# Gate's token shift through two identity products in PSUM, decay scan fed from PSUM, and new costs in the instruction scheduler

## The chip, the cores and the metric

The kernel runs on one core of a Trainium2 chip. A core has five engines with a queue of instructions each: PE multiplies matrices into PSUM (its weight loads are shown apart as PEld), DVE, ACT and POOL do elementwise work, SP issues the DMAs. Each engine takes its instructions strictly in the order in which they were written for it, and waits where an input isn't there yet. The metric is the device time of one execution in microseconds (us).

## The reference: what is computed

Two sequences of 512 and 256 tokens with 1024 channels go through the same two layers: a Mamba-2 layer and an RWKV-7 layer. The change touches the second only. Its parts that matter here:

```python
u = x @ w_in
u = u + (_token_shift_centred(u) - u) * mu        # 0.5 * (prev + next)
r, k, v = u[..., :R_DIM], ...
g = jax.nn.silu(u[..., 3 * R_DIM:4 * R_DIM])
...
w_log = -softplus(-(w0 + tanh(lw) @ w_up)) - 0.5
decay = exp(-exp(w_log))
...
out = (y + bonus) * g
```

The decays are multiplied along the tokens of a chunk; the kernel does that as a running sum of their logarithms.

## The kernel before, in words

The tokens of both sequences lie side by side (768 columns), the channels on the 128 partitions. All big products are split into three products of rounded parts (`mm3`, L144 to L146).

**Mamba stage** (up to about 760 us). It isn't edited.

**RWKV stage.** It works in 8 blocks `b` of 128 channels. For each block `rwkv_in` makes k, v, r and the gate g: a weight block is loaded and split (L125 to L127), `proj_cm` multiplies it with the input into one of two PSUM buffers `pj`, one for each sequence, and `shift_proj` does the token shift on the way out. ACT copies the buffer times `omu` = 1 - mu into SBUF (L741), and DVE adds the neighbours twice, once shifted by a token to the right and once to the left, each time reading PSUM and the SBUF result times `hmu` = mu / 2 (L743). For the gate, `omu` and `hmu` hold half of that, so that `in_g` can make silu from a tanh of the result (L840) and one more DVE instruction (L841). The gate then goes to DRAM (`sgd`) and is read again in `rwkv_final`, which multiplies it in (L1115).

`p1` goes through six windows of 256 tokens for a block. `p1_front` multiplies the low-rank parts into the PSUM bank `pl` (L873, L874), takes two tanh out of it (`ld` L877 and `ta` L878), scales `ld` in place in SBUF (L879), and DVE makes the running sum in place (the scan, L880); two exponentials follow. `pl` has one buffer. The front of a window runs one window ahead of `p1_back`, which makes the chunk matrices (L899 to L925).

`rwkv_inverse` inverts 24 triangles of 32 by 32 per block: some 60 dependent DVE instructions (L964, L965), two transposes (L967, L968), then the small products `tl` (L977), copies on ACT, the small products `px` (L987). `chain_step` runs the recurrence in 8 steps, and `rwkv_final` normalises a block's result: sums and products over `Y` on POOL (L1091 to L1101), then transposes `pf` on PE (L1105).

**What sets the order.** The order of the instructions on each engine isn't that of the code. `arrange` takes the whole program and schedules it as a list, with a cost for each instruction (`estimate`), a lag for each handover from one engine to the next (`HANDOVER`) and dependences (`trace`); it tries several settings and writes the best order found as fixed issue order. The projections of block b + 2 serve as filler on PE while block b goes through its chain. So a change of an instruction, a cost or a dependence can move instructions everywhere.

The two functions of the RWKV stage that the change edits most:

Of the kernel before, what the change touches and what calls it, by code (L numbers as in the profile page):

```python
# [14 lines left out]
F32 = mybir.dt.float32  # L15
# [3 lines left out]
AF = mybir.ActivationFunctionType  # L19
ALU = mybir.AluOpType  # L20
# [4 lines left out]
P = 128  # L25
# [16 lines left out]
DECAY = 0.5 * math.exp(-0.5)  # L42
# [6 lines left out]
def bc(ap, axis, n):  # L49
    a = ap.unsqueeze(axis)  # L50
    s = list(a.shape)
    s[axis] = n
    return a.to_broadcast(s)
# [6 lines left out]
class Trunk:  # L60
# [513 lines left out]
    def rwkv(self):  # L574
        nc, d = self.nc, self.d
        with ExitStack() as cx:
# [18 lines left out]
            self.hmu = rc.tile([P, 34], F32, name="hmu")  # L595
            nc.vector.tensor_scalar(self.omu, mu, -1.0, 1.0, op0=ALU.mult, op1=ALU.add)
            nc.vector.tensor_scalar_mul(self.hmu, mu, 0.5)
            for t in (self.omu, self.hmu):
                nc.vector.tensor_scalar_mul(t[:, 24:32], t[:, 24:32], 0.5)

            self.w0a0 = rc.tile([P, 4, RB], F32, name="w0a0")
            nc.vector.tensor_scalar_mul(self.w0a0, self.rpar[:, 0:4, :], 0.5)
# [19 lines left out]
            N = self.ring  # L622
# [110 lines left out]
    def shift_proj(self, j, out, seqs=(0, 1)):  # L733

        nc = self.nc
        ps = self.proj_cm(self.d["r_w_in"][j], seqs=seqs)
        for s in seqs:
            t0, n = SEQS[s]
            o = out[:, t0 : t0 + n]
            m = self.hmu[:, j : j + 1]  # L740
            nc.scalar.activation(o, ps[s], AF.Copy, scale=self.omu[:, j : j + 1])  # L741
            for a, p in ((o[:, 1:n], ps[s][:, 0 : n - 1]), (o[:, 0 : n - 1], ps[s][:, 1:n])):
                nc.vector.scalar_tensor_tensor(a, p, m, a, op0=ALU.mult, op1=ALU.add)  # L743
# [91 lines left out]
    def in_g(self, b):  # L835
        nc = self.nc
        g = self.t3("g")
        self.shift_proj(24 + b, g)
        th = self.t3("gth")
        nc.scalar.activation(th, g, AF.Tanh)  # L840
        nc.vector.scalar_tensor_tensor(th, th, 1.0, g, op0=ALU.add, op1=ALU.mult)  # L841
        nc.sync.dma_start(self.sgd[b], th)

# [19 lines left out]
    def p1_front(self, b, w, z, o, a, ps4, first):  # L863
        nc = self.nc
        col = lambda t, i: t[:, i, b : b + 1]
        w4 = lambda ap: ap.rearrange("p (c t) -> p c t", t=C)
        W = self.wt([P, 3, 256], "Wr")
        nc.sync.dma_start(W, self.ind[b, :, 0:3, a : a + 256])
        pl = self.pt("pl", [P, 2, 256], "pl")
        for i in range(2):  # L870
            wh, wl = self.wup
            x = self.lora_t[i][z][:, o : o + 256]
            nc.tensor.matmul(pl[:, i, :], wh[:, z, i, :], x, start=True, stop=False)  # L873
            nc.tensor.matmul(pl[:, i, :], wl[:, z, i, :], x, start=False, stop=True)  # L874
        ld = self.wt([P, 256], "ld")
        ta = self.wt([P, 256], "ta")
        nc.scalar.activation(ld, pl[:, 0, :], AF.Tanh, scale=0.5, bias=col(self.w0a0, z))  # L877
        nc.scalar.activation(ta, pl[:, 1, :], AF.Tanh, scale=0.5, bias=col(self.w0a0, 2 + z))  # L878
        nc.scalar.activation(ld, ld, AF.Copy, scale=-DECAY, bias=-DECAY)  # L879
        nc.vector.tensor_tensor_scan(ld, self.scanm, ld, 0.0, op0=ALU.mult, op1=ALU.add)  # L880
        EP = self.wt([P, 4, C + 1], "EP")
        nc.gpsimd.memset(EP[:, :, 0:1], 1.0)
        nc.scalar.activation(EP[:, :, 1:], w4(ld), AF.Exp)
        nc.scalar.activation(ld, ld, AF.Exp, scale=-1.0)
        return W, ld, ta, EP
# [197 lines left out]
    def rwkv_final(self, b, part=None):  # L1083

        nc, rw = self.nc, self.rw
        col = lambda i: self.rpar[:, i, b : b + 1]
        eng = nc.vector if b == RB - 1 else nc.gpsimd
        parts = range(3) if part is None else (part,)
        i0, n = 2 * parts[0], 2 * len(parts)
        y, sq = self.Y[:, i0 : i0 + n], self.Y[:, 6 + i0 : 6 + i0 + n]  # L1090
        eng.tensor_add(y, y, sq)  # L1091
        stat = lambda t: rw.tile([P, n, 2], F32, tag=t, bufs=1, name=t)
        mean, var = stat("gm"), stat("gv")
        nc.vector.tensor_reduce(mean, y, axis=AX.X, op=ALU.add)
        eng.tensor_scalar_mul(mean, mean, 1.0 / C)
        eng.tensor_sub(y, y, bc(mean, 3, C))
        nc.scalar.activation(sq, y, AF.Square)
        nc.vector.tensor_reduce(var, sq, axis=AX.X, op=ALU.add)
        nc.vector.tensor_scalar(var, var, 1.0 / C, GN_EPS, op0=ALU.mult, op1=ALU.add)
        rstd = self.rsqrt(rw, var, "ng")  # L1100
        eng.tensor_mul(y, y, bc(rstd, 3, C))  # L1101
        for k in parts:
            ps = self.pt("mi1", [P, 2, P], "pf")
            for i in range(2):
                nc.tensor.transpose(ps[:, i, :], self.Y[:, 2 * k + i].rearrange("p h v -> p (h v)"), self.ident)  # L1105
            o, bonus, g = (rw.tile([P, 2, P], F32, tag=t, bufs=1, name=t) for t in ("o", "bo", "sg"))
            r0, r1 = self.RGRP[k]
            tok = lambda ap: ap.rearrange("p (c t) -> p c t", t=P)[:, r0 : r1 + 1 : r1 - r0]
            oc = o.rearrange("p c (i t) -> p (c i) t", t=C)
            for i, dst in enumerate((oc[:, 0::2], oc[:, 3::-2])):  # L1110
                nc.scalar.activation(dst, ps[:, :, HR[i]], AF.Identity, scale=col(7), bias=col(8))
            nc.sync.dma_start(bonus, tok(self.bod[b]))
            nc.sync.dma_start(g, tok(self.sgd[b]))
            eng.tensor_add(o, o, bonus)
            nc.vector.tensor_mul(o, o, g)  # L1115
            if b == RB - 1:
                hi, lo = (tok(x[:, 1, :]) for x in self.x67)
                nc.scalar.copy(hi, o)
                nc.vector.tensor_sub(lo, o, hi.bitcast(F32))
            else:  # L1120
                nc.sync.dma_start(tok(self.odram[b]), o)
# [153 lines left out]
def size(ap, first=1):  # L1275
    return math.prod(int(n) for _, n in ap.ap[first:])
# [43 lines left out]
def space(t, name):  # L1320
    return str(t._space).endswith(name)


class Program:
# [49 lines left out]
    def estimate(self, i, x, src, dst):  # L1374
        e, op = self.eng[i], x.opcode
        if e == "SP":
# [4 lines left out]
            if dst:  # L1381
                n = size(dst[0], 0)
# [5 lines left out]
        if e == "PE":  # L1388
            N, M, K = size(src[0]), size(src[1]), int(src[0].ap[0][1])
# [30 lines left out]
        N = max(size(a) for a in src + dst)  # L1420
# [3 lines left out]
        ps = any(space(a.tensor, "PSUM") for a in src + dst if hasattr(a.tensor, "_space"))  # L1424
        ptr = sum(1 for a in src if size(a) == 1 and N > 1)
        two = len(src) - ptr
        if e == "DVE":
            if op != "TensorScalarPtr":
                c = (66 + N) / 0.96
                if op == "Reciprocal":  # L1430
                    c = 70 + N * 6.4
            elif x.ins and two == 1 and not ps:
                c = 69 + N / 1.92 + 61 * ptr
            else:
                c = (66 + N) / 0.96 + 61 * ptr
            if any(N > 64 and len(a.ap) > 1 and abs(int(a.ap[-1][0])) >= 16 and space(a.tensor, "SBUF") for a in src + dst):
                c += 0.78 * N
            if getattr(x, "is_tensor_tensor_scan", False):
                c = 70 + 2.07 * N
            if not ps:  # L1440
                self.lock[i] = c - 52
        elif e == "Activation":
            far = any(N > 64 and len(a.ap) > 1 and abs(int(a.ap[-1][0])) >= 16 for a in src + dst)
            c = 51 + N * (1.9 if far else 0.8333) + (0 if ps else 43) + 93.5 * ptr + (93 if len(dst) > 1 else 0)
        elif op == "Memset":
            c = 35 + 0.8333 * N
        elif op == "TensorScalarPtr":
            c = 130 + N * 0.83 + 90 * ptr
            self.lock[i] = c - 95
        elif two > 1:  # L1450
            c = 185 + 1.6 * N if N < 200 else 222 + 1.75 * N
            if str(x.outs[0].dtype) == "dt.float32r":
                c += 115
            self.lock[i] = c - 130
        else:
            c = 130 + 0.9 * N
            self.lock[i] = c - 87
        self.cost[i] = c

    def node(self, pred):  # L1460
# [7 lines left out]
    def trace(self, nc, tc, aps):  # L1468

        ins, eng = self.ins, self.eng  # L1470
# [12 lines left out]
        for i, x in enumerate(ins):  # L1483
# [17 lines left out]
            for wr, l in enumerate(aps[i]):  # L1501
                for b in l:
                    t = b.tensor
# [8 lines left out]
            for wr, nm, psum, q0, q1, bits in recs:  # L1512
                if nm in free_at:
                    pred.add(free_at[nm])
                W, R = live[nm]
                for j, a, z, m, w in chain(W, R) if wr or psum else W:
                    hit = a < q1 and q0 < z and m & bits
                    if psum or hit:
                        pred.add(j)
                        if eng[j] == eng[i] and w and hit:  # L1520
                            self.raw.add((j, i))
            for wr, nm, psum, q0, q1, bits in recs:
                W, R = live[nm]
# [409 lines left out]
```

## Time and profile before

| | |
|---|---|
| median of 3 runs | 1604.52 us (1603.03 to 1611.49) |
| the profiled execution | 1600.35 us, span 1598.5 us |
| mean granted PE clock | 0.978 |
| busy: PE, PEld, DVE, ACT, POOL | 94%, 79%, 84%, 54%, 45% |
| DMA | 161.41 MB, 101 GB/s over the span |
| chain of work that ended last | PE 67%, DVE 16%, POOL 6%, DMA 4%, ACT 3% |

How to read the lines that follow in this document. A group of instructions reads "line engine operation out<-in shape xcount | busy us, mean ns of one | idle time of the engine before them, and what ended it". A row of the timeline reads "start us, duration us, engine, line, operation, names, shape, count [idle before <- releaser]". A row of the waits reads "who waited <- for whom: us in total, times, longest". A row of the busy times by stretch reads "stretch, length, then the busy time and number of instructions of PE, PEld, DVE, ACT and POOL, the granted PE clock (1.00 is full), the share of the DMA engines, GB/s". A full fp32 product leaves two records on PE, a split one leaves one for each of its three parts. Durations overlap: a row of DVE holds some fixed time that the next instruction runs into.

### The profile page before, as it was taken

The page shows a single profiled execution, that of the slowest core. Times are in us where ns is not written, and L with a number is a line of the kernel's source. Part 1 is how long each engine was busy: PE and PEld are TensorE (multiplying, and loading weights), DVE is VectorE, ACT ScalarE, POOL GpSimd, SP SyncE. Part 2 cuts the span into 40 slices and gives each one's busy share as a digit, 9 for nine tenths or more (in the row PEclk, how much of TensorE's full clock was granted, in tenths as well). Part 3 has the DMA queues.
Part 4 walks back from the last instruction along what each step waited for, and adds up shares of the span by engine and source line. Part 5 has one row for each costly group of instructions (what it writes and reads, how often), then busy time and mean ns, then how long its engine had stood idle before and what let it go on. Part 6 is the DMA issues. An engine that isn't in the chain of part 4 may idle for free.

```text
span 1598.5 us, 39340 instructions
## 1 busy us (share of the span) xinstructions
PE 1497.7 (94%) x15210; PEld 1266.0 (79%) x15210; DVE 1340.6 (84%) x2947; ACT 857.1 (54%) x1988; POOL 712.0 (45%) x983
## 2 busy tenths in 40 slices
PE   7999999999999999999889989989999999988996
PEld 6878888888989779998768767777777777776886
DVE  6768988888978896569679788999999899989869
ACT  4245454544445453323565766757585766756342
POOL 1148574565754743000061644637283645547210
PEclk9999999999999999999989999999999999989998
DMA  5111212122012044432335334353535445345332
GB/s 174 54 46 36 78 34 67 60 70 84 28 66 80 14 139 133 134 120 80 106 106 160 111 101 140 105 149 86 149 92 141 121 114 153 100 139 156 111 114 87
DMA packets 150315, 161.41 MB, mean 101 GB/s; under 512 B 39632, under 2 KB 106928, under 8 KB 150128
## 3 DMA queue, kind: packets, MB, share of 16 engines
q1 hardware_dynamic: 150128, 158.89, 33.1%
q8 instruction: 120, 1.97, 0.5%
q14 instruction: 67, 0.55, 0.1%
HBM read 121.43 MB, written 40.55 MB: 101 GB/s over the span
## 4 chain that ended last, share of the span: by engine, by line
PE 67%; DVE 16%; POOL 6%; DMA 4%; issue 3%; ACT 3%; SPq 0%; DVEq 0%; POOLq 0%; ACTq 0%
PE pj L144 9%; PE pj L145 9%; PE pj L146 9%; PE pz L146 3%; PE pz L145 3%; PE pz L144 3%; PE po L146 3%; PE po L145 3%; PE po L144 3%; PE py L1040 2%; PE ptd L914 2%; PE pst L384 2%; PE py L423 2%; DVE tl L965 2%; DVE XN L964 2%
## 5 line engine op out<-in xcount | busy, mean ns | idle before, releaser
L144 PE MATMUL pj<-xh,whi 128*128 128x512 f32 (+1 forms) x1056 | 381.0, 361 | 20.3 <-ACT whi L126 11.7
L146 PE MATMUL pj<-xh,wlo 128*128 128x512 f32 (+1 forms) x1056 | 375.0, 356 | 1.6 <-DVE wlo L127 1.6
L145 PE MATMUL pj<-xl,whi 128*128 128x512 f32 (+1 forms) x1056 | 374.1, 354 | 1.1 <-DVE xl L140 1.1
L144 PEld LDWEIGHTS pj<-xh,whi 128*128 128x128 f32 x1056 | 205.0, 194 | 48.2 <-ACT whi L126 13.0
L146 PEld LDWEIGHTS pj<-xh,wlo 128*128 128x128 f32 x1056 | 204.4, 194 | 28.1 <-DVE wlo L127 3.0
L145 PEld LDWEIGHTS pj<-xl,whi 128*128 128x128 f32 x1056 | 204.7, 194 | 26.7 <-issue 2.7
L126 ACT CAST whi<-wraw 128x512 fp32r<-128x512 f32 x213 | 131.8, 620 | 135.2 <-PE pj L145 62.1
L127 DVE TENSOR_TENSOR wlo<-wraw,whi 128x512 fp32r<-128x512 f32 x213 | 157.9, 747 | 34.5 <-ACT whi L126 33.5
L418 POOL TENSOR_SCALAR G<-past,ddt,dt 128x128 f32<-128x128 f32 x192 | 136.0, 720 | 94.4 <-DVE ddt L324 59.2
L145 PE MATMUL po<-wlo,xh 128*128 128x256 f32 x528 | 150.7, 286 | 5.0 <-DVE wlo L127 5.0
L144 PE MATMUL po<-whi,xh 128*128 128x256 f32 x528 | 151.2, 286 | 0.1
L146 PE MATMUL po<-whi,xl 128*128 128x256 f32 x528 | 150.1, 284 | 0.0
L238 DVE SCALAR_TENSOR_TENSOR conv<-conv,convw 128x770 f32<-128x770 f32 x128 | 140.2, 1096 | 1.3
L144 PE MATMUL pz<-whi,xh 128*128 128x256 f32 x384 | 116.0, 302 | 0.4 <-DVE sz L262 0.4
L903 POOL TENSOR_TENSOR G<-EP,Wr 64x256 f32<-64x256 f32 x96 | 88.2, 919 | 51.2 <-DMA Wr<-ind 30.5
L146 PE MATMUL pz<-whi,xl 128*128 128x256 f32 x384 | 110.5, 288 | 0.0
L145 PE MATMUL pz<-wlo,xh 128*128 128x256 f32 x384 | 110.1, 287 | 0.0
L382 POOL TENSOR_TENSOR xw<-xB,dtws 128x256 f32<-128x256 f32 x64 | 54.1, 852 | 121.6 <-ACT xB L370 108.5
L145 PEld LDWEIGHTS po<-wlo,xh 128*128 128x128 f32 x528 | 100.1, 190 | 6.9 <-DVE wlo L127 5.9
L144 PEld LDWEIGHTS po<-whi,xh 128*128 128x128 f32 x528 | 100.2, 190 | 1.6 <-DVE acc L505 0.4
L146 PEld LDWEIGHTS po<-whi,xl 128*128 128x128 f32 x528 | 100.1, 190 | 1.1 <-issue 0.2
L1054 POOL TENSOR_TENSOR ZP<-SV,PC 64x128 f32<-64x128 f32 x128 | 64.9, 515 | 59.4 <-DVE SV L1066 48.4
(289 smaller groups left out, 3792.0 us busy)
## 6 DMA issues: line engine op xcount, KB each, us to landing
wraw<-in_r_w_in SPq DMA_DIRECT2D x72, 256.0 KB, 3.0
Wr<-ind SPq DMA_DIRECT2D x48, 384.0 KB, 3.8
wraw<-in_m_w_xbc SPq DMA_DIRECT2D x64, 256.0 KB, 2.8
wraw<-in_m_w_z SPq DMA_DIRECT2D x32, 256.0 KB, 2.8
wraw<-in_m_w_out SPq DMA_DIRECT2D x32, 256.0 KB, 4.6
ydram<-yst SPq DMA_DIRECT2D x16, 384.0 KB, 2.8
yraw<-ydram SPq DMA_DIRECT2D x24, 256.0 KB, 2.9
ind<-k SPq DMA_DIRECT2D x32, 192.0 KB, 3.0
```

Source lines behind the costliest of these rows:

```text
L126: nc.scalar.copy(hi, raw)
L127: nc.vector.tensor_sub(lo, raw, hi.bitcast(F32))
L144: mm(ps, ah, bh, start=first, stop=False)
L145: mm(ps, ah, bl, start=False, stop=False)
L146: mm(ps, al, bh, start=False, stop=last)
L238: nc.vector.scalar_tensor_tensor(acc, u[:, t : t + n], w[:, b, t : t + 1], acc, op0=ALU.mult, op1=ALU.add)
L382: nc.gpsimd.tensor_tensor(hv(xw), hv(xB[c][:, 0:256]), bc(self.dtws[:, c, z, hs], 2, 64), op=ALU.mult)
L384: nc.tensor.matmul(ps, xB[c][:, 256:384], xw, start=True, stop=True)
L418: nc.gpsimd.tensor_scalar(G[:, h, :], self.past, self.ddt[:, c, i : i + 1], self.dt[:, c, 0, i : i + 1], op0=ALU.mult, op1=ALU.add)
L423: nc.tensor.matmul(py[r, 64 * h : 64 * h + 64], G[:, h, r], x3[:, h, :], start=True, stop=True)
L903: nc.gpsimd.tensor_tensor(G[hr, ps4, h, 0, :], EP[hr, :, 0:C], w4(tok(W[hr, h])), op=ALU.mult)
L1054: nc.gpsimd.tensor_tensor(ZP[HR[h], :, s, :], SV[HR[h], :, s, h, :], bc(pc[s][HR[h]], 2, C), op=ALU.mult)
```

## The change

The gate's shift (and only the gate's: `j // 8 in (3,)`) takes another way. ACT copies the buffer times `hmu` into a piece `us` in SBUF. PE multiplies `us` with the identity and adds it into the same PSUM buffer, one token to the right, and again one token to the left. DVE then takes one pass: the buffer minus twice `us`. The gate is no longer halved on the way; the tanh gets a factor 0.5 and the last product in `rwkv_final` too. In `p1_front` the scaling of `ld` writes back into the bank `pl` instead of SBUF, and the scan reads it there. In the scheduler, costs of POOL instructions rise or change, and any two instructions on one engine other than PE that touch the same PSUM tile, the first of them writing, are now given the lag of a handover.

```diff
-            for t in (self.omu, self.hmu):
-                nc.vector.tensor_scalar_mul(t[:, 24:32], t[:, 24:32], 0.5)
...
+            if j // 8 in (3,):
+                u = self.inp.tile([P, n + 2], F32, tag=f"U{s}", bufs=1, name="us")[:, 0:n]
+                nc.scalar.activation(u, ps[s], AF.Copy, scale=m)
+                nc.tensor.matmul(ps[s][:, 1:n], self.ident, u[:, 0 : n - 1], start=False, stop=False, skip_group_check=True)
+                nc.tensor.matmul(ps[s][:, 0 : n - 1], self.ident, u[:, 1:n], start=False, stop=True, skip_group_check=True)
+                nc.vector.scalar_tensor_tensor(o, u, -2.0, ps[s], op0=ALU.mult, op1=ALU.add)
+                continue
...
-        nc.scalar.activation(th, g, AF.Tanh)
+        nc.scalar.activation(th, g, AF.Tanh, scale=0.5)
...
-        nc.scalar.activation(ld, ld, AF.Copy, scale=-DECAY, bias=-DECAY)
-        nc.vector.tensor_tensor_scan(ld, self.scanm, ld, 0.0, op0=ALU.mult, op1=ALU.add)
+        lp = pl[:, 0, :]
+        nc.scalar.activation(lp, ld, AF.Copy, scale=-DECAY, bias=-DECAY)
+        nc.vector.tensor_tensor_scan(ld, self.scanm, lp, 0.0, op0=ALU.mult, op1=ALU.add)
...
-            nc.vector.tensor_mul(o, o, g)
+            nc.vector.scalar_tensor_tensor(o, o, 0.5, g, op0=ALU.mult, op1=ALU.mult)
...
-            c = 35 + 0.8333 * N
+            c = 90 + 0.8333 * N
...
-            c = 185 + 1.6 * N if N < 200 else 222 + 1.75 * N
+            c = 185 + 1.6 * N if N < 200 else 240 + 1.8 * N
...
-                        if eng[j] == eng[i] and w and hit:
+                        if eng[j] == eng[i] and w and (hit or psum and eng[i] != "PE"):
```

Against before, line numbers behind L597 are lower by two, behind the gate's shift higher by five, and behind the scan higher by six (L977 is now L983).

How the order moves, at the end of the fifth inverse (the one whose `tl` starts at 1241.87 us in the profile before). PE, before: `pj_15031` and `pj_15056` are the gate's buffers for the two sequences, `pj_16118` is the next block's.

```order
L145 MATMUL pj_15056<-xl,whi 128x256
L146 MATMUL pj_15056<-xh,wlo 128x256
L144 MATMUL pj_15056<-xh,whi 128x256
L145 MATMUL pj_15056<-xl,whi 128x256
L146 MATMUL pj_15056<-xh,wlo 128x256
L977 MATMUL tl<-XN,TD 32x32 x48
L144 MATMUL pj_16118<-xh,whi 128x512
L145 MATMUL pj_16118<-xl,whi 128x512
```

PE, after the change, at the same place: `pj_15049` and `pj_15074` are the gate's buffers, `us` the scaled piece.

```order
L144 MATMUL pj_15074<-xh,whi 128x256
L145 MATMUL pj_15074<-xl,whi 128x256
L146 MATMUL pj_15074<-xh,wlo 128x256
L742 MATMUL pj_15049<-us,ident 128x511
L743 MATMUL pj_15049<-us,ident 128x511
L742 MATMUL pj_15074<-us,ident 128x255
L743 MATMUL pj_15074<-us,ident 128x255
L983 MATMUL tl<-XN,TD 32x32 x48
L144 MATMUL pj_16140<-xh,whi 128x512
L145 MATMUL pj_16140<-xl,whi 128x512
```

All four new products stand between the gate's last projection and `tl`. In the seven rounds with such a place this is so four times; in the others three, one or none of the four stand ahead of `tl` and the rest between `tl` and `px` (L993).

DVE at the same place, before, from the last transpose of the inverse on:

```order
L968 STREAM_TRANSPOSE TC<-tl 128x1024
L743 SCALAR_TENSOR_TENSOR g<-pj_15031,hmu,g 128x511
L127 TENSOR_TENSOR wlo<-wraw,whi 128x512
L743 SCALAR_TENSOR_TENSOR g<-pj_15031,hmu,g 128x511
L127 TENSOR_TENSOR wlo<-wraw,whi 128x512
L743 SCALAR_TENSOR_TENSOR g<-pj_15056,hmu,g 128x255 x2
L1115 TENSOR_TENSOR o<-o,sg 128x256
L900 TENSOR_TENSOR KB<-KB,Wr 128x2x4x64
```

DVE, after the change:

```order
L974 STREAM_TRANSPOSE TC<-tl 128x1024
L744 SCALAR_TENSOR_TENSOR g<-us,pj_15049 128x512
L127 TENSOR_TENSOR wlo<-wraw,whi 128x512
L744 SCALAR_TENSOR_TENSOR g<-us,pj_15074 128x256
L1121 SCALAR_TENSOR_TENSOR o<-o,sg 128x256
L846 SCALAR_TENSOR_TENSOR gth<-gth,g 128x768
L906 TENSOR_TENSOR KB<-KB,Wr 128x2x4x64
```

Two passes instead of four stand there, and the gate's last DVE instruction (L846) has moved up ahead of the next window's first (L906).

More of the change, by code (lines that the diff above doesn't have):

```diff
@@ L1450, in estimate @@
         elif two > 1:
-            c = 185 + 1.6 * N if N < 200 else 222 + 1.75 * N
+            c = 185 + 1.6 * N if N < 200 else 240 + 1.8 * N
             if str(x.outs[0].dtype) == "dt.float32r":
                 c += 115
-            self.lock[i] = c - 130
+            self.lock[i] = c - 170
         else:
-            c = 130 + 0.9 * N
-            self.lock[i] = c - 87
+            c = 190 + 0.9 * N
+            self.lock[i] = c - 147
         self.cost[i] = c
```

## The prediction, on record before the change was run

> **What bounds the kernel now.** I read the page's engine shares first, then the busy time by stretch, then the waits, then the timeline around one inverse.
>
> ```profile
> PE 1497.7 (94%) x15210; PEld 1266.0 (79%) x15210; DVE 1340.6 (84%) x2947; ACT 857.1 (54%) x1988; POOL 712.0 (45%) x983
> ```
>
> PE looks like the bound, but the share is an average over stages. By stretch (columns: PE, PEld, DVE, ACT, POOL busy, then granted clock, DMA share, GB/s):
>
> ```profile
> 0.00:570.00 570.00, 552.13 (x3895) 472.64 (x3896) 475.40 (x885) 267.57 (x571) 306.37 (x387) 1.00 0.20 64
> 850.00:1510.00 660.00, 610.69 (x8265) 487.06 (x8265) 599.06 (x1386) 429.63 (x1061) 332.42 (x487) 0.97 0.43 123
> 1115.20:1154.60 39.40, 35.68 (x314) 28.01 (x312) 37.34 (x115) 20.27 (x49) 9.84 (x15) 0.96 0.47 132
> 1154.60:1202.00 47.40, 46.94 (x845) 37.19 (x845) 42.39 (x73) 39.87 (x101) 34.45 (x55) 1.00 0.41 115
> 1202.00:1241.80 39.80, 35.28 (x305) 27.95 (x303) 38.01 (x116) 21.05 (x50) 11.62 (x16) 1.00 0.49 135
> 1241.80:1295.40 53.60, 52.02 (x842) 40.47 (x842) 45.48 (x76) 40.82 (x102) 39.90 (x59) 0.94 0.40 122
> ```
>
> The first row is the Mamba stage: PE 97% busy at full clock, and the change adds nothing there. The second is the RWKV loop, where all edits lie: PE 93%, DVE 91%. The other four are two of its eight rounds, each cut in two at the end of `rwkv_inverse`. During an inverse DVE is full (37.34 of 39.40, 38.01 of 39.80) and PE idles some 4 us; during the burst of windows and chain steps after it PE is full (46.94 of 47.40, 52.02 of 53.60) and DVE has 5 to 8 us to spare. So work taken from DVE pays during the inverse, and work given to PE costs in the burst. Which of the two the edits touch decides the sign.
>
> PE's idle time at the end of an inverse has two owners (us in total, times, longest):
>
> ```profile
> PE pf L1105 <- POOL Y L1101: 14.6, 7, 3.2
> PE tl L977 <- DVE TC L968: 4.7, 4, 1.8
> ```
>
> The second is the wait ahead of the `tl` products, which need the last transpose of the inverse. It is the only idle time that stands where the new products are put. One such place, PE:
>
> ```profile
> 1235.70 0.44 PE L1105 MATMUL pf<-ident,Y 128*128 128x128 f32 x2 [1.41 <-POOL Y L1101]
> ...
> 1240.30 0.28 PE L146 MATMUL pj<-xh,wlo 128*128 128x256 f32 x1
> 1241.87 2.00 PE L977 MATMUL tl<-XN,TD 32*32 32x32 f32 x96 [1.29 <-DVE TC L968]
> 1243.85 0.47 PE L144 MATMUL pj<-xh,whi 128*128 128x512 f32 x1
> 1244.15 0.40 PE L145 MATMUL pj<-xl,whi 128*128 128x512 f32 x1
> ...
> 1244.97 0.63 PE L145 MATMUL pj<-xl,whi 128*128 128x512 f32 x1
> 1245.39 0.63 PE L146 MATMUL pj<-xh,wlo 128*128 128x512 f32 x1
> ```
>
> and DVE at the same time:
>
> ```profile
> 1240.60 1.21 DVE L968 STREAM_TRANSPOSE TC<-tl 128x1024 f32<-128x1024 f32 x1
> 1241.73 0.71 DVE L743 SCALAR_TENSOR_TENSOR g<-pj,hmu,g 128x511 f32<-128x511 f32 x1
> ...
> 1244.22 0.99 DVE L743 SCALAR_TENSOR_TENSOR g<-pj,hmu,g 128x255 f32<-128x255 f32 x2
> 1245.13 0.41 DVE L1115 TENSOR_TENSOR o<-o,sg 128x256 f32<-128x256 f32 x1
> 1246.94 0.69 DVE L900 TENSOR_TENSOR KB<-KB,Wr 128x512 f32<-128x512 f32 x1 [1.39 <-DMA Wr<-ind]
> ```
>
> Here DVE does the gate's shift right behind the inverse, at the head of the burst, and then waits 1.39 us for a load.
>
> **The change part by part.** *Gate shift, DVE.* Rows: the two halves of the gate's shift, and the nearest row of the new form (SBUF and PSUM in, constant scalar, SBUF out).
>
> ```profile
> L743 DVE SCALAR_TENSOR_TENSOR g<-pj,hmu,g 128x511 f32<-128x511 f32 x16 | 11.7, 732 | 0.1
> L743 DVE SCALAR_TENSOR_TENSOR g<-pj,hmu,g 128x255 f32<-128x255 f32 x16 | 7.5, 471 | 3.2 <-ACT g L741 3.1
> L262 DVE SCALAR_TENSOR_TENSOR sz<-zth,pz 128x256 f32<-128x256 f32 x48 | 19.7, 410 | 1.3 <-ACT zth L260 1.0
> ```
>
> Removed: 11.7 + 7.5 = 19.2 us. Added: 8 of 256 columns at 410 ns and 8 of 512. A constant instead of a column of scalars is worth 471 - 410 = 61 ns, so 512 columns take about 732 - 61 = 671 ns; 8 x (671 + 410) = 8.7 us. DVE gains 10.5 us (9.6 if the 61 ns don't hold). ACT's copy is replaced one for one: 0.
>
> *Scan.* It took 759 ns on average.
>
> ```profile
> L880 DVE TENSOR_TENSOR_SCAN ld<-scanm,ld 128x256 f32<-128x256 bf16 x48 | 36.5, 759 | 3.3 <-ACT ld L879 2.8
> L442 DVE TENSOR_TENSOR yv<-yv,sz 128x256 f32<-128x256 f32 x48 | 23.6, 502 | 0.2
> L441 DVE TENSOR_TENSOR yv<-yv,py 128x256 f32<-128x256 f32 x48 | 19.8, 412 | 8.2 <-POOL yv L440 6.6 <-PE py L423 1.6
> ```
>
> The other two rows are the same product or sum of 256 columns with both inputs in SBUF (502) and with one in PSUM (412): 90 ns less. Between 0 and 90 ns for the scan, I take 83: 48 x 83 = 4.0 us (0 to 4.3). The Trainium skill, "SBUF — State Buffer", section "Who interferes with whom", gives a reason: DVE's second SBUF input comes through a read port shared with GpSimd, and an instruction with one SBUF input doesn't contend. By that rule the scan would get all of the 90 ns.
>
> Together DVE loses 14.5 us of work, 1.8 us a round. How much of it is time? The gate's part (10.5) is shed at the head of the burst, where DVE has idle time and PE none; the scans lie on both sides. I count half: -7 us (0 to -14.5).
>
> *Gate shift, PE.* Two products with the identity in full fp32 for each piece. A product of this kind leaves two records; the chain of waits shows four in 0.86 us for two products of 256 columns, so 0.43 each and 0.86 for 512; products standing alone with 64 rows take 1.05 and 0.63 (512 and 256 columns).
>
> ```profile
> 209.90 0.86 PE po L433 x4
> ...
> 85.20 1.05 PE prow L344 x2
> 87.27 0.63 PE prow L344 x2
> ```
>
> A round gets 2 x 0.86 + 2 x 0.43 = 2.58 us, eight rounds 20.6 us (26.9 at the dearer price). In the order, of the seven rounds with an inverse behind the gate, four have all four products straight ahead of `tl`, one has three (1.72), one a short one (0.43), one none; so 4 x 2.58 + 2.15 = 12.5 us stand ahead of `tl`, and 4.7 us of idle time is there to take them. The rest, 7.8 us, would make `tl` late. Those behind `tl` fill PE's wait for the copies that `px` needs: 0. What is queued behind a late `tl` is `px` and then the whole burst. But the copy out of PSUM and the sums go to PE earlier where the round's DVE work is shorter, so I take half, +4 us (0 to +7.8).
>
> *Clock.* In the PE rows above the spacing of 512-column products goes from 0.30 to 0.42 us, and their duration from 0.40 to 0.63, some 3 us after PE had stood idle for 1.41 and then 1.29 us. The burst's granted clock is 0.94 over 53.60 us: 3.2 us of PE work lost in that round; over the loop 0.03 x 660 = 20 us. Products that fill the idle time ahead of `tl` may avoid some of these drops. I take -3 us (0 to -10). The Trainium skill, "TensorE: Matmul & The Clock Gate", section "What's actually happening", has the half rate come after at least one idle window of about 3.4 us; by that rule no drop would have come here and nothing could be won. The trace disagrees: its idle pieces are shorter and the rate halves.
>
> *Wait added.* A window's `pl` bank is now held until the scan has read it, not until `ta` is made, and PE's next `pl` products stand behind that. One handover:
>
> ```profile
> 1163.11 0.48 ACT L878 ACTIVATE ta<-pl,w0a 128x256 f32<-128x256 f32 x1
> 1163.64 0.19 PEld L873 LDWEIGHTS pl<-lora,wuh 128*128 128x128 f32 x1
> 1163.92 0.69 DVE L880 TENSOR_TENSOR_SCAN ld<-scanm,ld 128x256 f32<-128x256 bf16 x1 [0.52 <-ACT ld L879]
> ...
> 1164.10 0.28 PE L874 MATMUL pl<-lora,wul 128*128 128x256 f32 x1
> ...
> 1165.00 0.47 ACT L877 ACTIVATE ld<-pl,w0a 128x256 f32<-128x256 f32 x1
> ```
>
> PE began the next window at 1163.64, 0.05 us after `ta`, and had it at 1164.38; the scan ended at 1164.61. So the next `pl` moves back by 1.0 us, to 1165.4, where ACT took it at 1165.00. The front runs one window ahead of the rest of its window, and that is the cover: 0. Without it, it is 1 us at each such handover.
>
> *The rest.* The copy into `pl` instead of SBUF, the constant in the last product with the gate, two setup multiplies: 0, none is on a full engine. The changed estimates reorder every engine. The Mamba stage can't gain, since PE is full; in the loop I put 0, between -5 and +5 us (a third of the 14.6 us that `pf` waits for POOL).
>
> Sum: -7 + 4 - 3 = **-6 us**. The profiled execution took 1600.35 us (span 1598.5), so 1594.3 for such a one; the median of the runs, 1604.5, lies 4.2 above it, so 1598.5.
>
> **The rivals.**
>
> *Full relief.* PE is late nowhere, because the clock stays up and the round is truly DVE's: all 14.5 us come off, 1590. For it: DVE's 95% during the inverses. Against it: the 1.39 us wait behind the gate's shift.
>
> *PE becomes the bound* (slower). The products sit in front of `tl` and the burst has no slack: 20.6 us added, 2 of them hidden in the 4.7, 7 won on DVE: +11.6, 1616. It decides where PE's idle time ahead of `tl` is under 2.6 us, as in every round (longest 1.8). Against it: four rounds only have all the products there.
>
> *The bank hold bites* (slower). The Trainium skill, "PSUM — Partial Sum Buffer", section "PSUM bank collisions raise a hardware error", forbids two engines in one bank and quadrant at once. In this kernel that means the `pl` products wait for the scan. If two of a round's six handovers cost 1 us and DVE delays those scans by half as much again, 8 x 2 x 1.5 = 24 us, less the 14.5 won on DVE: 1614. The trace speaks against it: even in the tight handover above ACT took the next `pl` only 0.4 us before the delayed products would end.
>
> *Nothing happens.* DVE's relief falls into its idle time and PE's products into PE's: 1604.5.
>
> **How the numbers follow.** Forecast 0.44, full relief 0.28, PE bound 0.16, bank hold 0.08, nothing 0.04. The forecast's own range is 1592 to 1606 (its terms at half their ends). A measurement tells about 0.5%, 8 us, from no change: the bounds are 1596.5 and 1612.5. Faster: full relief 0.28 and 0.3 of the forecast, 0.41. Slower: three quarters of PE bound and half of bank hold, 0.16. Same: 0.43. The range, 1586 to 1617, leaves out a fifth of full relief's cases below and the worst of both slow rivals above.
>
> **What would show it.** Right: in the loop DVE's busy time falls by 13 to 15 us and PE's idle time ahead of `tl` goes to about 0; the gate's group falls from 19.2 to 9 us; the scan from 759 to about 675 ns; the new products take 18 to 27 us of PE; the granted clock of the loop rises above 0.97. Wrong: `tl` starts over 2 us after its transpose (PE bound); PE waits for the scan at `pl` by over 10 us in total (bank hold); the Mamba stage changes by over 3 us.

## The result and the profile after

The changed kernel took 1594.68 us (median of 11 runs, 1589.23 to 1601.27), the kernel before 1603.03 in the same job (11 runs, 1599.86 to 1611.49). The ratio is 0.994, with a 95% interval of 0.9926 to 0.9954: by it 9.6 us faster, 7.4 to 11.9 (the two medians are 8.4 apart). The profiled execution took 1594.9 us, its span 1593.1. Of all runs counted here and below, one (1660.79 us, of the scan alone in the old order) was slow, at a lower granted clock (0.956), and is left out of the medians.

The first line is the busy time of the engines from the page of the changed kernel, the second its loop of rounds from the table by stretches (PE, PEld, DVE, ACT, POOL busy, then granted clock, DMA share, GB/s).

```profile
PE 1501.1 (94%) x15274; PEld 1272.7 (80%) x15274; DVE 1327.4 (83%) x2929; ACT 862.2 (54%) x1988; POOL 687.2 (43%) x983
```

```profile
850.00:1510.00 660.00, 618.61 (x8424) 495.04 (x8426) 590.26 (x1375) 436.42 (x1068) 320.29 (x487) 0.98 0.43 124
```

DVE has 13.2 us less work than before (1340.6). PE is as full as it was, with 64 more records, which are 32 products, and the loop's clock stands at 0.98 after 0.97. ACT's first copy of a token shift in the RWKV stage starts at 761.8 us (761.1 before), so the Mamba stage is no shorter. The two profiled spans differ by 5.4 us. This gain lies in the loop (its last inverse ends at 1504.6, before at 1508.2) and in the tail behind it (1.8 us shorter).

The groups of the edited lines in the loop (x14 of a product are two records each for seven rounds):

```profile
L886 DVE TENSOR_TENSOR_SCAN ld<-scanm,pl 128x256 f32<-128x256 bf16 x42 | 28.4, 676 | 1.9 <-ACT pl L885 1.6
...
L885 ACT ACTIVATE pl<-ld 128x256 f32<-128x256 f32 x42 | 16.3, 387 | 0.8
...
L743 PE MATMUL pj<-us,ident 128*128 128x511 f32 x14 | 7.3, 607 | 0.0
...
L744 DVE SCALAR_TENSOR_TENSOR g<-us,pj 128x512 f32<-128x512 f32 x7 | 4.6, 657 | 0.0
...
L743 PE MATMUL pj<-us,ident 128*128 128x255 f32 x14 | 4.3, 386 | 0.0
...
L744 DVE SCALAR_TENSOR_TENSOR g<-us,pj 128x256 f32<-128x256 f32 x7 | 2.8, 400 | 0.0
```

The scan takes 676 ns instead of 759, ACT's copy ahead of it 387 instead of 421, and the gate's sums 7.4 us in seven rounds, which is 8.5 in eight, instead of 19.2. PE's waits in the loop (us in total, times, longest):

```profile
PE pf L1111 <- POOL Y L1107: 9.0, 6, 2.8
...
PE pl L878 <- DVE ld L886: 3.2, 5, 1.6
...
PE tl L983 <- DVE TC L974: 2.1, 3, 1.5
```

The wait ahead of `tl` is down from 4.7 us and that of `pf` from 14.6, and the new wait for the scan at `pl` is small.

### The profile page after: what moved, and what is told of

Read it like the earlier page. It is cut to its first block, busy times and chain, and to the rows that moved or that the text cites. A ratio compares the mean times of both kernels' runs of the same rounds, so it can differ in the third digit from the quotient of the medians.

```text
span 1593.1 us, 39443 instructions
## 1 busy us (share of the span) xinstructions
PE 1501.1 (94%) x15274; PEld 1272.7 (80%) x15274; DVE 1327.4 (83%) x2929; ACT 862.2 (54%) x1988; POOL 687.2 (43%) x983
## 4 chain that ended last, share of the span: by engine, by line
PE 70%; DVE 16%; POOL 4%; ACT 4%; DMA 2%; issue 2%; SPq 1%; DVEq 0%; ACTq 0%; POOLq 0%
PE pj L144 10%; PE pj L145 10%; PE pj L146 10%; PE po L144 3%; PE po L145 3%; PE po L146 3%; PE pz L145 3%; PE pz L144 3%; PE pz L146 3%; PE ptd L920 3%; PE py L1046 2%; PE pst L384 2%; DVE tl L971 2%; DVE XN L970 2%; PE po L433 2%
## 5 line engine op out<-in xcount | busy, mean ns | idle before, releaser
L146 PE MATMUL pj<-xh,wlo 128*128 128x512 f32 (+1 forms) x1056 | 370.5, 351 | 7.2 <-DVE wlo L127 7.2
L418 POOL TENSOR_SCALAR G<-past,ddt,dt 128x128 f32<-128x128 f32 x192 | 127.5, 677 | 93.1 <-DVE ddt L324 60.1
L1060 POOL TENSOR_TENSOR ZP<-SV,PC 64x128 f32<-64x128 f32 x128 | 61.6, 489 | 63.8 <-DVE SV L1072 48.1
```

The lines of the kernel that those rows point to most:

```text
L146: mm(ps, al, bh, start=False, stop=last)
L418: nc.gpsimd.tensor_scalar(G[:, h, :], self.past, self.ddt[:, c, i : i + 1], self.dt[:, c, 0, i : i + 1], op0=ALU.mult, op1=ALU.add)
L1060: nc.gpsimd.tensor_tensor(ZP[HR[h], :, s, :], SV[HR[h], :, s, h, :], bc(pc[s][HR[h]], 2, C), op=ALU.mult)
```

## The experiments

At the start there were three theories. A: the operations gain, by VectorE's (DVE's) relief. B: the changed estimates gain, by the order they make. C: the identity products fill TensorE's (PE's) idle time and keep its clock up. Each run has its ratio to the kernel before on the same chip; the runs stand on three chips. "Slower" below means that the whole interval of the ratio lies above 1.

### Each part alone, in an order planned for it

Four kernels take parts of the change, and the scheduler plans each anew.

**Gate's shift alone** (scan and estimates as before):

```diff
+            if j // 8 in (3,):
...
+                nc.tensor.matmul(ps[s][:, 1:n], self.ident, u[:, 0 : n - 1], start=False, stop=False, skip_group_check=True)
+                nc.tensor.matmul(ps[s][:, 0 : n - 1], self.ident, u[:, 1:n], start=False, stop=True, skip_group_check=True)
+                nc.vector.scalar_tensor_tensor(o, u, -2.0, ps[s], op0=ALU.mult, op1=ALU.add)
```

> The kernel before with the gate's new shift alone; the scan and the estimates as they were. Theory A (the gain is VectorE's relief, the gate's shift giving most of it): VectorE's busy time over the span falls by 9 to 10.5 us, the eight gates' group from 19.2 to about 9 us, and the time falls by 4 to 7 us, to 1596 to 1599. Theory B (the gain comes from the order that the new estimates make): no gain, 1603 within 3 us, since the identity products cost TensorE what VectorE is spared. Theory C (the identity products fill TensorE's idle time and keep the granted clock up): a gain of 4 to 8 us with a loop clock above 0.97.

Measured: 1613.9 us, ratio 1.0063 (1.0041 to 1.0084). Slower.

**Scan from PSUM alone:**

```diff
-        nc.scalar.activation(ld, ld, AF.Copy, scale=-DECAY, bias=-DECAY)
-        nc.vector.tensor_tensor_scan(ld, self.scanm, ld, 0.0, op0=ALU.mult, op1=ALU.add)
+        lp = pl[:, 0, :]
+        nc.scalar.activation(lp, ld, AF.Copy, scale=-DECAY, bias=-DECAY)
+        nc.vector.tensor_tensor_scan(ld, self.scanm, lp, 0.0, op0=ALU.mult, op1=ALU.add)
```

> The kernel before with the scan's input in PSUM alone. Theory A: the scan falls from 759 to about 676 ns and ScalarE's copy ahead of it from 421 to about 387 ns, 4.0 and 1.6 us of work, and the time falls by 1 to 4 us, to 1599 to 1602. Theories B and C: no change, 1603 within 2 us. If the longer hold of the pl bank cost time, it would be slower, by 2 to 5 us.

Measured: 1609.4 us, ratio 1.0033 (1.0019 to 1.0046). Slower. The size is the one expected of a longer bank hold, but PE waits only 3.2 us in the loop for scans at `pl`, as much as in the changed kernel.

**Changed estimates alone** (only the scheduler's costs and its dependence rule):

```diff
-            c = 35 + 0.8333 * N
+            c = 90 + 0.8333 * N
...
-            c = 130 + 0.9 * N
+            c = 190 + 0.9 * N
```

> The kernel before with the changed estimates alone: the same instructions in another order. Theory A: no change, 1603 within 3 us. Theory B: the whole of the gain, 1594 to 1597, with TensorE's wait for GpSimd ahead of pf down from 14.6 to about 9 us as in the changed kernel.

Measured: 1613.5 us, ratio 1.0056 (1.004 to 1.0072). Slower, with the very instructions of the kernel before. PE's wait for POOL ahead of `pf` is 14.8 us in the loop, not the 9 that theory B expected.

**Gate's shift and scan, with the old estimates** (the edits in the scheduler undone):

```diff
-            c = 190 + 0.9 * N
+            c = 130 + 0.9 * N
...
```

> The changed kernel with the estimates put back: gate shift and scan together in an order made by the old estimates. Theory A: the whole of the gain, 1593 to 1597. Theory B: 1600 to 1603. Theory C: 1595 to 1599, with a loop clock of 0.98 against 0.97.

Measured: 1611.8 us, ratio 1.0038 (1.0025 to 1.0052). Slower.

All three theories miss here: every part alone is slower, and so are both edits without the estimates, yet the whole is 0.6% faster. What each kernel changes besides its operations is the order of everything. The same instructions in two orders differ by 9 us (estimates alone against the kernel before), the changed operations in two orders by 16 us (1.0038 against 0.994). So a part can't be judged while the scheduler plans anew. Nor does the gate's edit raise the clock in every order: over the whole program its mean is 0.970 to 0.980 in the executions of the gate alone, 0.969 to 0.979 with gate, scan and the old estimates, and 0.976 to 0.982 in the kernel before.

### Operations and order apart

The next kernels don't plan. They have an order written out as a table, taken from one of the two kernels, so that operations and order are changed one at a time:

```diff
-    for line in prog.schedule().values():
+    for line in issue_order():
```

Where an edit has other instructions than the order's own kernel, they stand in its place: the one sum where the second of the two stood, two sums where the one stood, the products where ACT's copy lands by the planned times. With the scan's input in PSUM, PE's next products into `pl` move back behind the scan where the old order has them ahead of it.

**Both edits in the order of the kernel before:**

> The operations of the changed kernel (gate shift and scan) in the issue order of the kernel before, written out as a table; the identity products stand where their copy lands, and TensorE's order gives way only where the pl bank demands it. Theory A (the operations gain, by VectorE's relief, and what each planned order is worth is another matter): 1592 to 1599. Theory B (the new order gains, the operations do not): 1601 to 1607.

Measured: 1645.0 us, ratio 1.0249 (1.0228 to 1.027). Neither range holds it.

**No edit, in the order of the changed kernel:**

> The operations of the kernel before in the issue order of the changed kernel, instruction by instruction (the two sums of each gate piece stand where the one sum stood). Theory A: no gain, 1601 to 1609. Theory B: the whole gain, 1593 to 1597.

Measured: 1610.3 us, ratio 1.0034 (1.0021 to 1.0047). Theory B falls: for the old operations the new order is worse than the old one, by 5.5 us. Theory A's range is passed by 1.3 us.

**Gate's shift alone in the order of the changed kernel:**

> The changed kernel in its own issue order with the scan put back to SBUF. Theory A, with the scan worth its 4.0 us on VectorE and 1.6 us on ScalarE times a share of half to all: 1597 to 1600. Theory B: 1594 to 1596.

Measured: 1606.0 us, ratio 1.0009 (0.9996 to 1.0022), above both ranges.

**Scan alone in the order of the changed kernel:**

> The changed kernel in its own issue order with the gate's shift put back (two sums on VectorE, no identity products). Theory A, with the gate worth 10.5 us of VectorE's work times half, less up to 4 us of TensorE's: 1597 to 1603. Theory B: 1594 to 1596.

Measured: 1604.0 us, ratio 1.0003 (0.9987 to 1.0019), 1 us above theory A's range.

**Gate's shift alone in the order of the kernel before:**

> The gate's shift alone in the issue order of the kernel before, the identity products standing where their copy lands. The run with both edits in that order took 1645.0 us. If the products do the harm there (an order that left little idle time ahead of tl), most of it is here: 1620 to 1645. If the scan does, through the pl bank, this one is near the kernel before or a little faster by VectorE's relief: 1597 to 1606.

Measured: 1617.7 us, ratio 1.0072 (1.0047 to 1.0097), between the two expectations. The busy time of the engines in this run:

```profile
PE 1515.6 (94%) x15274; PEld 1273.9 (79%) x15274; DVE 1333.9 (83%) x2929; ACT 856.8 (53%) x1988; POOL 715.5 (44%) x983
```

PE is busy 17.9 us longer than in the kernel before (1497.7) and idles only 3.4 us less (97.4 of a span of 1613.0, against 100.8 of 1598.5), so the new products aren't covered. `tl` isn't where it shows: it starts at most 1.7 us after its transpose, 3.9 us in all over eight rounds. In six of seven rounds the two short products stand behind `tl`, in four of these behind `px` too, and the seven bursts behind `tl` take 354.1 us instead of 343.0.

**Scan alone in the order of the kernel before:**

> The scan from PSUM alone in the issue order of the kernel before, which let TensorE write the next pl before the scan of the last had run; there TensorE's rows now give way. If the longer hold of the bank is what cost 40 us in the run with both edits in that order: 1625 to 1645, with TensorE's wait for the scan at pl over 10 us. If not: 1599 to 1604 by the shorter scans.

Measured: 1637.0 us, ratio 1.0198 (1.0156 to 1.0241). The longer hold of the bank is most of what costs. PE's wait for it from 850 to 1510 us shows that (the last inverse of this run ends at 1541):

```profile
PE pl L873 <- DVE ld L881: 17.9, 21, 3.4
```

PE waits 21 times for the scan, where the changed kernel waits 5 times; over the whole execution it is 21.8 us. PE idles 122.7 us in all, 21.9 more than in the kernel before. The old order let the next products into `pl` follow close behind `ta`, and now they stand behind the scan, which on average ends 2.2 us after `ta`. Put together, the ratios to the kernel before are:

| order | no edit | gate | scan | both |
|---|---|---|---|---|
| of the kernel before | 1 | 1.0072 | 1.0198 | 1.0249 |
| of the changed kernel | 1.0034 | 1.0009 | 1.0003 | 0.9940 |

In the new order the edits gain 0.94%, or 15.1 us (0.9940 / 1.0034); in the old one they lose 2.5%. Of two kernels that share this order, then, the one with the edits is faster: the gain is that of the operations in an order that was planned around them. In the new order the gate gains 4.0 us alone and 10.1 beside the scan; the scan 5.0 alone and 11.1 beside the gate. By the intervals each of these is known within about 3 us.

### What the operations gain in the new order

First, what the identity products do to PE. This is PE's timeline with no edit in the new order, third round, around `tl` (start, length, and in brackets the idle time before and who ended it):

```profile
1063.43 0.39 PE L146 MATMUL pj<-xh,wlo 128*128 128x512 f32 x1
1064.61 2.01 PE L977 MATMUL tl<-XN,TD 32*32 32x32 f32 x96 [0.80 <-DVE TC L968]
1066.55 0.44 PE L1105 MATMUL pf<-ident,Y 128*128 128x128 f32 x2
1068.83 2.02 PE L987 MATMUL px<-TC,TL 32*32 32x32 f32 x96 [1.84 <-ACT TL L980]
1072.00 0.79 PE L144 MATMUL pj<-xh,whi 128*128 128x512 f32 x1 [1.15 <-DVE g L743]
1072.59 0.63 PE L145 MATMUL pj<-xl,whi 128*128 128x512 f32 x1
1073.02 0.63 PE L146 MATMUL pj<-xh,wlo 128*128 128x512 f32 x1
```

The same place in the changed kernel:

```profile
1060.76 0.40 PE L146 MATMUL pj<-xh,wlo 128*128 128x512 f32 x1
1061.00 0.59 PE L742 MATMUL pj<-us,ident 128*128 128x255 f32 x2
1061.52 2.00 PE L983 MATMUL tl<-XN,TD 32*32 32x32 f32 x96
1063.45 0.70 PE L743 MATMUL pj<-us,ident 128*128 128x255 f32 x2
1063.99 1.02 PE L742 MATMUL pj<-us,ident 128*128 128x511 f32 x2
1064.84 1.02 PE L743 MATMUL pj<-us,ident 128*128 128x511 f32 x2
1065.70 0.38 PE L1111 MATMUL pf<-ident,Y 128*128 128x128 f32 x2
1066.01 1.99 PE L993 MATMUL px<-TC,TL 32*32 32x32 f32 x96
1067.94 0.50 PE L144 MATMUL pj<-xh,whi 128*128 128x512 f32 x1
1068.27 0.39 PE L145 MATMUL pj<-xl,whi 128*128 128x512 f32 x1
1068.50 0.40 PE L146 MATMUL pj<-xh,wlo 128*128 128x512 f32 x1
```

Without the products PE idles three times here, for 0.80, 1.84 and 1.15 us; the last of these is for the gate's second sum on DVE, which still reads the buffer. With them there is no gap: one stands ahead of `tl`, three between `tl` and `px`. Behind it the 512-column products follow each other every 0.23 us instead of every 0.43. The clock is that of the stretches: with no edit in the new order, the loop and then the 15.4 us behind `tl` of this round,

```profile
850.00:1510.00 660.00, 599.44 (x8114) 480.73 (x8113) 600.20 (x1358) 428.72 (x1055) 330.44 (x484) 0.95 0.43 122
1064.60:1080.00 15.40, 12.39 (x254) 9.81 (x258) 11.07 (x17) 12.43 (x24) 9.50 (x13) 0.67 0.60 188
```

and in the changed kernel the same stage of the round:

```profile
1060.50:1076.00 15.50, 15.50 (x307) 11.76 (x306) 11.83 (x20) 14.49 (x30) 10.14 (x15) 1.00 0.66 212
```

The clock is 0.67 against 1.00 there, and 0.95 against 0.98 over the loop. The loop of the scan alone, in the new order,

```profile
850.00:1510.00 660.00, 602.04 (x8130) 484.00 (x8129) 590.52 (x1366) 430.21 (x1055) 318.15 (x485) 0.95 0.42 122
```

and of the gate's shift alone, in the new order:

```profile
850.00:1510.00 660.00, 615.24 (x8229) 490.90 (x8229) 593.75 (x1371) 428.40 (x1057) 335.24 (x486) 0.98 0.43 123
```

In this order it is the gate's edit that brings the clock back. All executions agree: over the whole program their mean clocks are 0.967 to 0.973 with no edit, 0.967 to 0.974 with the scan alone, 0.976 to 0.982 with the gate alone and 0.979 to 0.987 with both. The busy time of the engines with no edit in the new order:

```profile
PE 1494.2 (93%) x15210; PEld 1270.3 (79%) x15210; DVE 1349.7 (84%) x2947; ACT 861.5 (54%) x1988; POOL 701.8 (44%) x983
```

In a span of 1608.2 us PE idles 114.0; in the changed kernel it idles 92.0 of 1593.1 (1501.1 busy). So the edits take away 22.0 us of its idle time, and the new products, some 20 us, make it only 6.9 us busier. Added up from the timeline, PE is idle for 21.9 us in the 8 us ahead of the eight `tl` with no edit, for 7.9 us in the changed kernel. PE's wait for `tl` alone, with no edit in the new order:

```profile
PE tl L977 <- DVE TC L968: 12.1, 5, 4.0
```

Two runs ask which half of the gate's edit counts, and how much room is left.

**Identity products doubled** (each piece is scaled with a quarter instead of half, and each product issued twice):

```diff
-                nc.scalar.activation(u, ps[s], AF.Copy, scale=m)
+                nc.scalar.activation(u, ps[s], AF.Copy, scale=self.qmu[:, j : j + 1])
                 nc.tensor.matmul(ps[s][:, 1:n], self.ident, u[:, 0 : n - 1], start=False, stop=False, skip_group_check=True)
+                nc.tensor.matmul(ps[s][:, 1:n], self.ident, u[:, 0 : n - 1], start=False, stop=False, skip_group_check=True)
+                nc.tensor.matmul(ps[s][:, 0 : n - 1], self.ident, u[:, 1:n], start=False, stop=False, skip_group_check=True)
                 nc.tensor.matmul(ps[s][:, 0 : n - 1], self.ident, u[:, 1:n], start=False, stop=True, skip_group_check=True)
-                nc.vector.scalar_tensor_tensor(o, u, -2.0, ps[s], op0=ALU.mult, op1=ALU.add)
+                nc.vector.scalar_tensor_tensor(o, u, -4.0, ps[s], op0=ALU.mult, op1=ALU.add)
```

> The changed kernel in its own issue order, each identity product issued twice in a row on half the input, the same sum. TensorE gets what it already got from the change once more, about 20 us by the prediction's price of 2.58 us a round. If the products lie in idle time of TensorE that still has room (the wait for tl): 1593 to 1598. If that room is used up and each further product delays tl and what is queued behind it: 1605 to 1615.

Measured: 1609.3 us, ratio 1.0022 (0.9997 to 1.0046), 13.2 us over the changed kernel (1.0022 / 0.9940). The room is used up. PE's timeline of the fifth round, whose `TC` was ready at 1248.2:

```profile
1248.12 1.02 PE L747 MATMUL pj<-us,ident 128*128 128x511 f32 x2
1248.97 0.59 PE L744 MATMUL pj<-us,ident 128*128 128x255 f32 x2
1249.40 0.59 PE L745 MATMUL pj<-us,ident 128*128 128x255 f32 x2
1249.83 0.59 PE L746 MATMUL pj<-us,ident 128*128 128x255 f32 x2
1250.26 0.59 PE L747 MATMUL pj<-us,ident 128*128 128x255 f32 x2
1250.79 2.00 PE L987 MATMUL tl<-XN,TD 32*32 32x32 f32 x96
```

The products stand 0.85 and 0.43 us apart, and `tl` starts 2.6 us after its transpose. Over the eight rounds `tl` is 10.0 us late, against 2.0 in the changed kernel. That is 8.0 us more; the other 5 of the 13 aren't located.

**The gate's one sum made twice** (products stay, DVE gets work back):

```diff
                 nc.vector.scalar_tensor_tensor(o, u, -2.0, ps[s], op0=ALU.mult, op1=ALU.add)
+                nc.vector.scalar_tensor_tensor(o, u, -2.0, ps[s], op0=ALU.mult, op1=ALU.add)
```

> The changed kernel in its own issue order with each gate piece's one sum on VectorE made twice in a row, the second over the first: TensorE's identity products stay, and 8 x (676 + 381) = 8.5 us of the VectorE work that the change took away come back. Theory A (relief of VectorE is what gains): most of the gate's part goes again, 1600 to 1605. Theory C (the identity products fill TensorE's idle time ahead of tl and keep its granted clock up): little goes, 1594 to 1598, and the loop's clock stays at 0.98.

Measured: 1601.0 us, ratio 0.9974 (0.9953 to 0.9996), 5.5 us over the changed kernel for 8.5 us of DVE's work. By the two intervals the 5.5 us are known within 4.1, so the share is 0.64, but anything from 0.16 to 1.1 fits. The stretch behind `tl` of the third round, in this run:

```profile
1062.00:1077.40 15.40, 15.40 (x307) 11.70 (x306) 12.89 (x21) 14.45 (x30) 9.97 (x15) 1.00 0.66 213
```

The clock stays at 1.00 here and at 0.98 over the loop, so it hangs on the products and not on DVE's relief. With the share of 0.64, the 10.5 us that the gate takes off DVE are worth 6.7, within 5; of the 10.1 us that the gate brings beside the scan, 3.4 remain for the filled gaps and the clock, less what the products cost. By these bounds that rest could be nothing. So in the new order theory A holds; of theory C the filled gaps and the clock are shown, their worth in time isn't; and B, that the order gains by itself, falls.

## Why the prediction was right or wrong

The sum was -6 us and the time fell by 9.6 (0.6% of 1603.03), to a point inside the range. Several terms under the sum do not hold.

**DVE's work, right.** 14.5 us less was forecast, 13.2 is measured over the span. The gate's group went to 8.5 us (8.7 forecast), the scan to 676 ns (676 forecast). The share, put at half, measures 0.64 for the gate's part, between 0.16 and 1.1.

**The scan's part was sized in the wrong order.** In the new order an SBUF scan would take not 759 but 810 ns, so the edit is worth 6.4 us there and not 4.0, besides 1.6 on ACT's copy, which the sum didn't have at all.

**PE's products, the price right, the cover wrong.** 2.58 us a round holds (0.85 and 0.43 us a product, above). But `tl` became late by 2.0 us in all against 1.6 before, not by 4 more. The step that failed is "4.7 us of idle time is there to take them": that counts only waits for `TC` in the order of the kernel before. By the count of all idle time in the 8 us ahead of `tl` the old order has 15.7 us, and the new one without the products 21.9. One round also differs from what the text ahead of the prediction says: where `tl` starts at 1148.94 us, none of the four products stands ahead of it, one stands between `tl` and `px`, and three stand behind `px`, 1.72 us in the burst for which the sum has no term. In the old order the edit alone takes 1617.7 us, near the 1616 of the rival "PE becomes the bound". The heart of that rival, PE's added work without cover, is what the run shows; its way, over a late `tl`, is not, since `tl` is late by 3.9 us in all. The order decides between this rival and the forecast.

**The bank hold at 0, right only for an order that knows of it.** The changed kernel waits 3.2 us for scans at `pl`. In the old order, with the scan alone, it is 17.9 us between 850 and 1510 us and 21.8 in all, and that edit costs 2.0%, or 32 us, where the rival had put 24. What was wrong is the evidence against this rival: one handover was taken for all, and in the old order PE waited 24 times. The 32 us are, in the profiled executions, 21.9 us more idle time of PE and 10.4 us more busy time for the same number of products (1508.1 against 1497.7), at a clock of 0.974 against 0.978.

**The clock, right in kind.** -3 us was for a rise above 0.97; it is 0.98. In the new order it is 0.95 without the gate's edit and 0.98 with it. What it is worth by itself wasn't measured apart from the gaps. The rule of the Trainium skill ("TensorE: Matmul & The Clock Gate", section "What's actually happening"), an idle window of about 3.4 us ahead of the half rate, would have no drop in the third round above, whose gaps are at most 1.84 us; the clock there is 0.67, and the measurement decides. Between these gaps stand only `tl`, `px` and one `pf`; whether such small products count for the clock no run here tests.

**The rest, wrong in size.** "In the loop I put 0, between -5 and +5 us" was the worst step. The estimates alone cost 9 us. The new order costs the old operations 5.5, and the changed operations differ by 16 us between the orders of the old and new estimates. With that term put right, the sum is +5.5 for the order and -15.1 for the operations in it: the forecast's -6 is near the result because it mis-sized both, in opposite directions, and that is luck. This is one way through the table of ratios; the other way, the operations in the old order cost 39.9 us and the new order takes 49.5 off again, so neither part has a price of its own. "Full relief" (1590, -14.5 for the operations) is the rival that comes nearest to what the operations do, with the order's price left out.

**Still open.** Why gate and scan gain 4.0 and 5.0 us apart and 15.1 together; the excess of 6.1 is known within 4.5. The profiles put it near the end. From the first to the seventh `tl` the new order takes 540.5 us with no edit, 534.1 with the gate, 533.9 with the scan and 528.7 with both: gains of 6.3, 6.6 and 11.8, which nearly add. But in its last round the scan alone loses 4.4 us (96.9 against 92.5), and there PE is busy without a break from 1480 to 1490 us at a granted clock of 0.50. That execution (1609.5 us) is one of the longer ones of its run (1602.3 to 1609.7). What holds the clock down there isn't shown. Also open is whether the new estimates plan better or drew a good order: three orders of the old operations span 0.56%, and other draws for the new ones weren't run. None of the kernels run is faster than the changed one.

## What to carry to other kernels

Where a scheduler plans the order, an edit and its order are one change: an edit timed alone after a new plan tells mostly of the plan, so write the order out as a table and change one of the two at a time. Work that is moved to a full engine is judged by the gaps at its new place in the new order, and there it may pay twice, by the work taken off the other engine and by gaps that no longer lower the clock (here 0.95 against 0.98 over the loop; what that alone is worth wasn't separated). A buffer that is held longer costs little in an order planned with it (3.2 us of waits here) and a lot in one that was not (21.8 us).

## What the runs showed of the hardware

A scan with both inputs in SBUF is not one price. The no-edit kernel in the new order, then the changed kernel (min/median/max ns):

```profile
L880 DVE TENSOR_TENSOR_SCAN ld<-scanm,ld x48: 669/683/1217, 794.7 to 1464.2; 128x256 f32<-128x256 bf16 x48
```

```profile
L886 DVE TENSOR_TENSOR_SCAN ld<-scanm,pl x48: 664/674/689, 795.3 to 1451.6; 128x256 f32<-128x256 bf16 x48
```

The medians are 9 ns apart, and the mean of 810 comes from 16 scans of 753 to 1217 ns. All 16 lie beside a two-input product or sum on POOL (in the kernel before, 10 of 48, all beside one); but 14 others lie beside one too and take less, so not every such neighbour costs. Of the 48 scans from PSUM 33 lie beside one, and none takes more than 689. The Trainium skill, "SBUF — State Buffer", section "Who interferes with whom", says that the second SBUF input goes through a port shared with GpSimd; the rows agree. So the 83 ns of the prediction were no fixed price: the edit removes a stall that depends on what POOL does meanwhile.
